# Round 0 keeps the weights' block sums of 14 quads in DRAM, and round 1 loads them

## The chip, the cores and the metric

The kernel runs on one core of one Trainium2 chip. The metric is device time in microseconds (us) of one execution, lower is better; it is given as the median of several runs. TensorE (PE in the profile) does the matmuls, VectorE (DVE), ScalarE (ACT) and GpSimd (POOL) the elementwise work, and SyncE (SP) issues nearly all DMAs, one after the other, in the order in which they stand in its queue.

## The reference

One layer: RMS norm, one input projection to eight groups of 512 columns, a gated short convolution on four of the groups, chunkwise retention with rotary positions on the other four, one output projection with a residual, and a last RMS norm. The sequence has 2048 positions behind 16 learned ones, the model is 1024 wide. Cut to what matters here:

```python
def mixer_layer(h, norm_g, w_in, conv_w, ret_norm_g, w_out, pos):
    hn = rms_norm(h, norm_g)
    proj = jnp.einsum('bld,de->ble', hn, w_in)          # 1024 -> 8*512
    cx, cb, cc, cg, q, k, v, rg = jnp.split(proj, N_PROJ, axis=-1)
    conv_out = short_conv_branch(cx, cb, cc, conv_w) * jax.nn.silu(cg)
    ...
    ret = head_group_norm(retention_chunkwise(qf, kf, vf), ret_norm_g)
    ret_out = ret.astype(h.dtype) * jax.nn.silu(rg)
    mixed = jnp.concatenate([conv_out, ret_out], axis=-1)
    return h + jnp.einsum('ble,ed->bld', mixed, w_out)
```

All of it is float32.

## The kernel before

**Rounds and units.** The 2048 positions are done in two rounds of 1024. A round has eight units: four heads of the retention (units 0 to 3, `head`) and four groups of convolution channels (units 4 to 7, `conv_group`). Round 0 goes through them in the order 4, 0, 1, 2, 3, 5, 6, 7, round 1 in the order 0 to 7. A unit has two quads, so a round has 16. After round 1 come eight pairs of the output projection (`output`).

**A quad.** A quad multiplies a 256 x 1024 piece of the weights by the 1024 x 1024 piece of x. Weights and x are each cut into 2 x 2 blocks, and the product is made in Strassen's way (the form of Winograd): seven block products instead of eight. For the weights' side that takes the four blocks a11, a12, a21, a22 (128 x 512 each, 256 KB) and four sums of them. Function `stationary` makes these in place with one addition and three subtractions: s1 = a21 + a22, a21 = a11 - a21, a11 = s1 - a11, a12 = a12 - a11. It does so on GpSimd, with one exception, the first quad of unit 0 in round 0, which DVE does. The seven left sides, in order, are a11, a12, the new a11, s1, the new a21, the new a12, a22. The weights are the same in both rounds, so before the change both rounds load the same four blocks and make the same sums.

**Split in two parts.** Each float32 operand is split into a high part (a cast on ACT to the format that TensorE takes, line 119, tile wh) and a low part (a subtraction on DVE, line 120, tile wl). Each of the seven products is 4 x 3 matmuls of 128 x 128 by 128 x 512 (line 246). The parts of the weights go through rings of 3 tiles, so the cast of one product's weights waits until PE is through with the product three places back.

**Slots.** The blocks loaded (tile ra) and s1 (tile sa) share a ring of 8 slots (`RAW`), 5 per quad. A block's load waits until the block that had the slot 8 places before is read for the last time, as a rule by its split.

**x and its sums.** The sums on the side of x are made once per round, and those for round 1 are made ahead in round 0 and kept in DRAM (`sums_x`); so are those of the output weights (`sums_w`). The first unit of round 0 (unit 4) and the first quad of unit 0 in round 1 don't use sums: they do eight plain block products (lines 327 and 303), since the sums of x aren't there yet.

**The order.** The program is written unit by unit; a scheduler then fixes one order of instructions for each engine and for SP's queue, which the chip keeps to. On SP stand, beside the weights' loads (line 542), the transposes by DMA of k, v and the retention's output (line 721, tiles pl, tr, apart, across), the loads of x, and stores of results (`mixed`, line 550). In a head, v and k go through such a transpose, are copied by ACT (lines 823 and 814), weighed (line 829) and multiplied (line 862). In round 0 the products of the 16 learned positions (line 500) read the first quad's raw blocks, so that the sums in place wait for them.

Of the kernel before, what the change touches and what calls it, by code (L numbers as in the profile page):

```python
# [8 lines left out]
F32 = mybir.dt.float32  # L9
F32R = mybir.dt.float32r  # L10
# [5 lines left out]
P = 128  # L16
# [4 lines left out]
NG = 4  # L21
EPS = 1e-6
HB = 512
# [55 lines left out]
def hybrid_trunk(ctx: ExitStack, tc: tile.TileContext, t, out: bass.AP, chunk_decay):  # L79
# [36 lines left out]
    def split(hi, lo, src, scale=None, eng=nc.vector):  # L116

        if scale is None:
            nc.scalar.copy(out=hi, in_=src)  # L119
            lowered[0] = eng.tensor_tensor(out=lo, in0=src, in1=hi.bitcast(F32), op=ALU.subtract)  # L120
            return
        scaled[0] = nc.scalar.mul(hi, src, scale)  # L122
        nc.vector.scalar_tensor_tensor(  # L123
            out=lo, in0=src, scalar=scale, in1=hi.bitcast(F32), op0=ALU.mult, op1=ALU.subtract
        )
# [12 lines left out]
            tiles.append(a)  # L138
        return tiles

    def stationary(blocks, eng=nc.gpsimd):

        a11, a12, a21, a22 = blocks
        s1 = sb.tile([P, HB], F32, name="sa", tag="ra", bufs=RAW)

        def parts(src):
            hi = sb.tile([P, HB], F32R, name="wh", tag="wh", bufs=RING)
            lo = sb.tile([P, HB], F32R, name="wl", tag="wl", bufs=RING)
            split(hi, lo, src)
            return hi, lo  # L150

        w = [parts(a11), parts(a12)]
        add(eng, s1, a21, a22)
        sub(eng, a21, a11, a21)
        sub(eng, a11, s1, a11)
        sub(eng, a12, a12, a11)
        w.append(parts(a11))
        third[0] = lowered[0]
        w += [parts(a) for a in (s1, a21)]
        fifth[0] = lowered[0]  # L160
        return w + [parts(a) for a in (a12, a22)]

    def operand(i, kt):
# [71 lines left out]
    def quad(w, m, take, steps=()):  # L235


        steps = iter(steps)

        def product(i, bank, first):  # L240
            (wh, wl) = w[i]
            for kt in range(KH):
                ks = slice(kt * P, (kt + 1) * P)
                mh, ml = m[i][kt]
                for n, (a, b) in enumerate(((wl, mh), (wh, ml), (wh, mh))):
                    nc.tensor.matmul(  # L246
                        bank, a[:, ks], b, start=first and kt == 0 and n == 0, stop=kt == KH - 1 and n == 2,
                        skip_group_check=not first,
                    )

        def copy(bank):
            c = sb.tile([P, HB], F32, name="tc", tag="tc", bufs=COPIES)
            copied[0] = nc.scalar.copy(out=c, in_=bank)  # L253
            return c

        def step():
            with tc.issue_after(copied[0].ins):
                next(steps, lambda: None)()

        xb = ps_proj()  # L260
        product(0, xb, True)
        c = copy(xb)
        step()
        yb = ps_proj()
        product(1, yb, True)
        take(0, 0, yb, c)
        product(2, xb, False)
        u2 = copy(xb)
        step()
        zb = ps_proj()  # L270
        product(3, zb, True)
        c = copy(zb)
        step()
        product(4, xb, False)
        take(1, 1, xb, c)
        product(5, zb, False)
        take(0, 1, zb, u2)
        product(6, xb, False)
        take(1, 0, xb, None)
# [258 lines left out]
        nc.tensor.transpose(tp[:, :NMETA], u, ident[:NMETA, :NMETA])  # L538
        nc.vector.tensor_copy(out=conv_carry[g], in_=tp[:, NMETA - 2 : NMETA])

    def w_loads(n):
        return [lambda a, i=i: nc.sync.dma_start(a, t["w_in"][n, i]) for i in range(4)]

    mixed = [
        dram.tile([2, 2, 2, P, KH, P], F32, name=f"mixed{b}", tag=f"mixed{b}") for b in range(SEQ // HB)
# [87 lines left out]
    def conv_group(g, r, m, f, blocks, ahead, steps=(), last=False):  # L633


        def go_on():
            next(factors_ahead[0], None)

        def behind(quad, *own):
            return [lambda n=n: (own[n](), go_on() if (quad, n) in steps else None) for n in range(3)]  # L640

        u = [gen("u") for _ in range(2)]
        rr, rr2 = ([a[:, j * HB : (j + 1) * HB] for j in range(2)] for a in f[:2])
        held = [None]

        def mul(eng, out, a, b):
            eng.tensor_tensor(out=out, in0=a, in1=b, op=ALU.mult)  # L647

        def take(i, j, pp, c):
            s = u[j][:, 2:]  # L650
            if c is None:
                mul(nc.vector, s, pp, s)
            elif i == 1:
                add(nc.vector, c, pp, c)
                held[0] = c
            else:
                add(nc.vector, s, pp, c)
                mul(nc.vector, s, s, rr2[j])
                if j == 1:
                    mul(nc.gpsimd, s, s, held[0])  # L660

        blocks, meta = blocks
        quad(stationary(blocks), m, take, behind(0, finish_late, idle, idle))
        catch_up(0)
        if meta:
            meta_carry(g, meta)
        carry(u, g, r)
        cs = [taps(u[j], g) for j in range(2)]
        gates = []

        def gated():
            j, c = gates.pop()
            nc.scalar.activation(c, c, AF.Silu)  # L673
            mul(nc.gpsimd, cs[j], cs[j], rr[j])
            mul(nc.gpsimd, cs[j], cs[j], c)

        def take(i, j, pp, c):
            if i == 0:
                add(nc.vector, c, pp, c)
                mul(nc.vector, c, c, rr[j])  # L680
                gates.append((j, c))
                if j == 1:
                    gated()
                return
            if c is not None:
                add(nc.vector, c, pp, c)
                pp = c
            taken[0] = nc.vector.tensor_tensor(out=cs[j], in0=pp, in1=cs[j], op=ALU.mult)

        n = 2 * (NG + g) + 1  # L690
        quad(stationary(load_raw(w_loads(n))), m, take, behind(1, idle, gated, idle))
        blocks = ahead()
        def store():
            for j in range(2):
                store_mixed(r, j, g, cs[j])

        if last:
            kept.append(store)
        else:
            store()  # L700
        return blocks
# [47 lines left out]
    def head(h, r, m, rot_t, f, turning, blocks, ahead, sums, first=(), between=((), idle, idle, idle)):  # L749
# [26 lines left out]
        if len(first) > 0:  # L776
            quad_plain(first[0], m, take)
        else:
            with tc.issue_after(spreading[0].ins) if r + h == 0 else nullcontext():
                w = stationary(blocks[0], nc.vector if r + h == 0 else nc.gpsimd)  # L780
            quad(w, m, take, between[0] or (finish_late,))
            catch_up(0)
        between[1]()
# [53 lines left out]
            join_keys(0)  # L837
            between[3]()

        quad(stationary(load_raw(w_loads(2 * h + 1))), m, take, (split_late, middle, late_middle))  # L840
        with tc.issue_after(copied[0].ins):
            join(1)
            weigh(1)
# [185 lines left out]
    def ahead(r, n, early=False):  # L1029

        if n is None:
            return None
        blocks = load_raw(w_loads(2 * n))
        return blocks, meta_products(blocks, early) if r == 0 else None

    warm_up(WARM)
# [171 lines left out]
```

## Time and profile before

| | |
|---|---|
| median of 3 runs | 865.88 us (865.87 to 866.58) |
| profiled execution | 866.67 us |
| its span, first to last instruction | 864.9 us |
| granted TensorE clock, mean | 0.999 |
| PE, DVE, ACT, POOL busy | 99%, 83%, 58%, 43% |
| DMA | 129.51 MB, mean 150 GB/s |

The busy time of an engine is a share of the whole span. A matmul's record lasts about 390 ns, but the records overlap, so PE's pace is read from how many matmuls start in a stretch. Round 0 ends at about 350 us, round 1 at about 700 us. In rows of groups the columns are: line, engine, operation, tiles written and read, shape, count, then busy time and mean of one (ns), then idle time of the engine ahead of them with what ended it. In rows of a timeline the first two numbers are the start in the span and the length, both in us. In rows of windows the stretch comes first, then its length, then busy time and count of PE, weight loads, DVE, ACT and POOL, then the granted clock, the share of the DMA engines and GB/s. In rows of the chain: start, length, what.

### The profile page before, as it was taken

The numbers are of one execution on the slowest core, as the hardware profiler recorded it, in microseconds if no ns is written. First come the engines' busy times: TensorE is split into PE (matmuls) and PEld (weight loads), VectorE is DVE, ScalarE is ACT, GpSimd is POOL, SyncE is SP. The second block draws the span as 40 slices with busy tenths as digits, with TensorE's granted clock in tenths as the row PEclk, the third lists the DMA queues.
The fourth block names the chain that finished last, engine by engine and source line by source line (L and its number), as shares of the span: only waits on it lengthen the run. The fifth ranks groups of instructions, "written<-read, shape, count | busy, mean of one in ns | idle before, by whom it ended". The sixth has DMA issues, their size and how long they took to land.

```text
span 864.9 us, 12698 instructions
## 1 busy us (share of the span) xinstructions
PE 854.6 (99%) x4216; PEld 705.6 (82%) x4216; DVE 716.8 (83%) x1204; ACT 499.4 (58%) x901; POOL 374.0 (43%) x278
## 2 busy tenths in 40 slices
PE   9999999999999999999999999999999999999996
PEld 6778888878887878788888888888888888788885
DVE  6798989889897977989789898988767799877663
ACT  7875648474855654948284757534433566555553
POOL 0022232423245554452232424364746455677773
PEclk9999999999999999999999999999999999999999
DMA  9724246454656533945264637546132584555441
GB/s 299 255 87 100 60 97 161 112 146 135 158 172 193 195 98 98 332 143 135 62 158 128 165 122 156 173 122 207 51 84 74 185 314 137 168 165 182 152 135 73
DMA packets 127506, 129.51 MB, mean 150 GB/s; under 512 B 58384, under 2 KB 76112, under 8 KB 127440
## 3 DMA queue, kind: packets, MB, share of 16 engines
q1 hardware_dynamic: 126864, 128.30, 49.9%
q8 instruction: 33, 0.54, 0.3%
q10 hardware_dynamic: 576, 0.40, 0.2%
q14 instruction: 33, 0.27, 0.1%
HBM read 90.91 MB, written 25.17 MB: 134 GB/s over the span
## 4 chain that ended last, share of the span: by engine, by line
PE 91%; DVE 4%; DMA 3%; issue 1%; ACT 1%; SPq 0%; POOLq 0%; POOL 0%; DVEq 0%
PE pj L246 73%; PE pj L303 5%; PE pj L327 5%; PE ms L886 2%; PE ms L875 2%; PE ms L885 2%; PE ms L862 2%; DVE wl L120 1%; PE ms L500 1%; DVE ml L120 1%; DMA ra<-in_w_in 1%; DMA w<-in_w_out 1%; DMA x<-in_xT 1%; DMA sums_w<-w 1%; DVE yo L128 0%
## 5 line engine op out<-in xcount | busy, mean ns | idle before, releaser
L246 PE MATMUL pj<-mh,wl 128*128 128x512 f32 x1008 | 395.7, 393 | 0.7 <-DVE yo L961 0.6
L246 PE MATMUL pj<-mh,wh 128*128 128x512 f32 x1008 | 393.2, 390 | 0.0
L246 PE MATMUL pj<-ml,wh 128*128 128x512 f32 x1008 | 392.7, 390 | 0.0
L119 ACT CAST wh<-ra 128x512 fp32r<-128x512 f32 x216 | 134.1, 621 | 230.8 <-PE pj L246 193.8
L120 DVE TENSOR_TENSOR wl<-ra,wh 128x512 fp32r<-128x512 f32 x216 | 192.6, 893 | 41.6 <-ACT wh L119 40.7
L246 PEld LDWEIGHTS pj<-mh,wl 128*128 128x128 f32 x1008 | 189.3, 188 | 41.8 <-issue 1.6
L246 PEld LDWEIGHTS pj<-mh,wh 128*128 128x128 f32 x1008 | 189.2, 188 | 39.5
L246 PEld LDWEIGHTS pj<-ml,wh 128*128 128x128 f32 x1008 | 189.3, 188 | 37.9
L131 POOL TENSOR_TENSOR ra<-ra 128x512 f32<-128x512 f32 x70 | 115.0, 1642 | 102.6 <-PE ms L500 51.7
L128 POOL TENSOR_TENSOR sa<-ra 128x512 f32<-128x512 f32 x35 | 53.1, 1518 | 100.1 <-DVE wl L120 42.5
L131 POOL TENSOR_TENSOR ra<-sa,ra 128x512 f32<-128x512 f32 x35 | 49.4, 1412 | 82.6 <-DVE wl L120 76.1
L253 ACT COPY tc<-pj 128x512 f32<-128x512 f32 x108 | 62.7, 581 | 0.1
L898 POOL TENSOR_TENSOR rp<-rs,neg_half 128x4 f32<-128x4 f32 x16 | 19.0, 1185 | 45.3 <-DVE rs L128 45.2
L961 DVE TENSOR_TENSOR yo<-pj,yo 128x512 f32<-128x512 f32 (+1 forms) x33 | 22.0, 671 | 16.3 <-PE pj L246 8.7
L972 POOL TENSOR_TENSOR z<-yo,final_g 128x512 f32<-128x512 f32 x16 | 27.4, 1714 | 18.6 <-DVE yo L961 18.6
L647 POOL TENSOR_TENSOR c<-c,tc 128x512 f32<-128x512 f32 x14 | 24.5, 1747 | 20.3 <-ACT tc L673 20.1
L119 ACT CAST wh<-sa 128x512 fp32r<-128x512 f32 x36 | 22.3, 619 | 18.3 <-PE pj L246 18.0
L647 POOL TENSOR_TENSOR c<-c,rr 128x512 f32<-128x512 f32 x14 | 24.1, 1718 | 19.9 <-DVE c L565 10.0
L902 DVE TENSOR_SCALAR pm<-ms,mv,rp 128x128 f32<-128x128 f32 x64 | 21.8, 404 | 10.2 <-POOL rp L898 10.2
L123 DVE SCALAR_TENSOR_TENSOR ml<-x,gain,mh 128x512 fp32r<-128x512 f32 x32 | 25.6, 836 | 5.5 <-ACT mh L122 5.4
L128 DVE TENSOR_TENSOR tc<-pj,tc 128x512 f32<-128x512 f32 x28 | 19.2, 686 | 13.1 <-PE pj L246 13.0
L120 DVE TENSOR_TENSOR wl<-sa,wh 128x512 fp32r<-128x512 f32 x36 | 27.9, 775 | 1.0 <-ACT wh L119 1.0
(161 smaller groups left out, 1256.3 us busy)
## 6 DMA issues: line engine op xcount, KB each, us to landing
ra<-in_w_in SPq DMA_DIRECT2D x124, 256.0 KB, 2.8
x<-in_xT SPq DMA_DIRECT2D x48, 256.0 KB, 5.1
w<-in_w_out SPq DMA_DIRECT2D x32, 256.0 KB, 4.9
ra<-mixed SPq DMA_DIRECT2D x32, 256.0 KB, 2.7
yo<-in_x SPq DMA_DIRECT2D x32, 256.0 KB, 4.6
ra<-in_x SPq DMA_DIRECT2D x16, 256.0 KB, 3.2
mixed<-c SPq DMA_DIRECT2D x16, 256.0 KB, 2.4
sums_x<-x SPq DMA_DIRECT2D x16, 256.0 KB, 2.7
```

The costliest lines, as they stand in the source:

```text
L119: nc.scalar.copy(out=hi, in_=src)
L120: lowered[0] = eng.tensor_tensor(out=lo, in0=src, in1=hi.bitcast(F32), op=ALU.subtract)
L123: nc.vector.scalar_tensor_tensor(out=lo, in0=src, scalar=scale, in1=hi.bitcast(F32), op0=ALU.mult, op1=ALU.subtract)
L128: eng.tensor_tensor(out=out, in0=a, in1=b, op=ALU.add)
L131: eng.tensor_tensor(out=out, in0=a, in1=b, op=ALU.subtract)
L246: nc.tensor.matmul(bank, a[:, ks], b, start=first and kt == 0 and n == 0, stop=kt == KH - 1 and n == 2, skip_group_check=not first,)
L253: copied[0] = nc.scalar.copy(out=c, in_=bank)
L303: nc.tensor.matmul(banks[i], a[:, ks], b, start=half + kt + n == 0, stop=half == 1 and kt == KH - 1 and n == 2,)
L327: nc.tensor.matmul(banks[n][i], a[:, ks], b, start=half + kt + s == 0, stop=half == 1 and kt == KH - 1 and s == 2,)
L647: eng.tensor_tensor(out=out, in0=a, in1=b, op=ALU.mult)
L961: last[0] = nc.vector.tensor_tensor(out=y[:, cs], in0=pp[:, cs], in1=y[:, cs], op=ALU.add)
L972: nc.gpsimd.tensor_tensor(out=ys[i][j], in0=y, in1=final_g[:, j * HB : (j + 1) * HB], op=ALU.mult)
```

## The change

Of the 16 quads of a round, all but the two of unit 4 are "kept" (`KEPT`, 14 quads). In round 0, `stationary` gets a place in DRAM for such a quad and, once its four sums are made, stores them there: 4 DMAs of 256 KB per quad, 56 in all, from SP. In round 1 a kept quad loads seven blocks, a11, a12, the four sums, and a22, and `stationary` only splits them: no addition or subtraction on GpSimd. The sums then aren't in a tile of their own (sa) but come in slots of the ring (ra), seven per quad instead of five. The two quads of unit 4 in round 1 still load four blocks and make their sums. The first quad of unit 0 is stored as the others are, but in round 1 it is the plain one and loads its four raw blocks, so 13 quads load sums. Lines move by up to 16 (542 is 555 in the changed kernel, 721 is 737, 550 is 566).

```diff
+    def weight_parts(src):
+        hi = sb.tile([P, HB], F32R, name="wh", tag="wh", bufs=RING)
+        lo = sb.tile([P, HB], F32R, name="wl", tag="wl", bufs=RING)
+        split(hi, lo, src)
+        return hi, lo
+
+    def stationary(blocks, eng=nc.gpsimd, keep=None):
+
+        if len(blocks) > 4:
+            return [weight_parts(a) for a in blocks]
         a11, a12, a21, a22 = blocks
         s1 = sb.tile([P, HB], F32, name="sa", tag="ra", bufs=RAW)
...
         w += [parts(a) for a in (s1, a21)]
         fifth[0] = lowered[0]
+        if keep is not None:
+            for i, a in enumerate((a11, s1, a21, a12)):
+                nc.sync.dma_start(keep[i], a)
         return w + [parts(a) for a in (a12, a22)]
...
-    def w_loads(n):
-        return [lambda a, i=i: nc.sync.dma_start(a, t["w_in"][n, i]) for i in range(4)]
+    sums_a = dram.tile([4 * NG, 4, P, HB], F32, name="sums_a", tag="sums_a")
+    KEPT = [n for n in range(4 * NG) if n // 2 != NG]
+
+    def w_loads(n, r=0):
+        if r and n in KEPT:
+            blocks = t["w_in"][n, 0], t["w_in"][n, 1], *(sums_a[n, i] for i in range(4)), t["w_in"][n, 3]
+        else:
+            blocks = [t["w_in"][n, i] for i in range(4)]
+        return [lambda a, b=b: nc.sync.dma_start(a, b) for b in blocks]
+
+    def kept_sums(n, r):
+        return sums_a[n] if r == 0 and n in KEPT else None
...
-        quad(stationary(load_raw(w_loads(n))), m, take, behind(1, idle, gated, idle))
+        quad(stationary(load_raw(w_loads(n, r)), keep=kept_sums(n, r)), m, take, behind(1, idle, gated, idle))
```

The calls in `conv_group`, `head` and `ahead` pass the round and the place in the same way.

Up to round 1 the order on PE, DVE, ACT and POOL is unchanged; SP's queue gets the stores. SP in the head of unit 1 in round 0, before (tr and pl are v and k on their way through the transpose):

```order
L542 DMA ra<-in_w_in 128x512 x3
L721 DMA_TRANSPOSE across<-apart 128x8x128
L721 DMA_TRANSPOSE tr<-pl 128x8x128
L542 DMA ra<-in_w_in 128x512
L721 DMA_TRANSPOSE tr<-pl 128x8x128
L721 DMA_TRANSPOSE across<-apart 128x8x128
L721 DMA_TRANSPOSE tr<-pl 128x8x128
L542 DMA ra<-in_w_in 128x512 x2
L721 DMA_TRANSPOSE tr<-pl 128x8x128
```

and the same place now:

```order
L555 DMA ra<-in_w_in 128x512 x3
L737 DMA_TRANSPOSE across<-apart 128x8x128
L166 DMA sums_a<-ra 128x512 x2
L737 DMA_TRANSPOSE tr<-pl 128x8x128
L555 DMA ra<-in_w_in 128x512
L737 DMA_TRANSPOSE tr<-pl 128x8x128
L737 DMA_TRANSPOSE across<-apart 128x8x128
L737 DMA_TRANSPOSE tr<-pl 128x8x128
L166 DMA sums_a<-sa 128x512
L555 DMA ra<-in_w_in 128x512 x2
L737 DMA_TRANSPOSE tr<-pl 128x8x128
```

Two stores of sums stand between the first two transposes, and one ahead of the two loads. SP from the end of round 0 into round 1, before (n are rows of x for the norm, x the blocks of round 1, t their sums):

```order
L402 DMA n<-in_x 128x512 x2
L542 DMA ra<-in_w_in 128x512 x4
L464 DMA x<-in_xT 128x512 x16
L227 DMA t<-sums_x 128x512 x3
L542 DMA ra<-in_w_in 128x512
```

and now:

```order
L408 DMA n<-in_x 128x512 x2
L166 DMA sums_a<-sa 128x512
L166 DMA sums_a<-ra 128x512
L555 DMA ra<-in_w_in 128x512 x3
L166 DMA sums_a<-ra 128x512 x2
L555 DMA ra<-in_w_in 128x512
L470 DMA x<-in_xT 128x512 x16
L233 DMA t<-sums_x 128x512 x3
L555 DMA ra<-in_w_in 128x512
```

The four stores of round 0's last quad stand among the loads of round 1's first weights, two of them ahead of the last such load and the 16 loads of x. SP in the first quads of round 1, where the loads of sums come in, before:

```order
L721 DMA_TRANSPOSE tr<-pl 128x8x128 x2
L542 DMA ra<-in_w_in 128x512 x2
L721 DMA_TRANSPOSE tr<-pl 128x8x128
L542 DMA ra<-in_w_in 128x512 x2
L721 DMA_TRANSPOSE tr<-pl 128x8x128
L542 DMA ra<-in_w_in 128x512 x7
```

and now:

```order
L737 DMA_TRANSPOSE tr<-pl 128x8x128 x2
L555 DMA ra<-in_w_in 128x512 x2
L737 DMA_TRANSPOSE tr<-pl 128x8x128
L555 DMA ra<-sums_a 128x512 x4
L737 DMA_TRANSPOSE tr<-pl 128x8x128
L555 DMA ra<-in_w_in 128x512 x3
L555 DMA ra<-sums_a 128x512 x4
L555 DMA ra<-in_w_in 128x512 x2
```

The loads of raw blocks a21 are gone, four loads of sums stand in their place, and they are ahead of the last transpose of unit 0.

More of the change, by code (lines that the diff above doesn't have):

```diff
@@ L139, in load_raw @@
         return tiles
-    def stationary(blocks, eng=nc.gpsimd):
+    def weight_parts(src):
[6 more added lines that the diff above has]
+            return [weight_parts(a) for a in blocks]
         a11, a12, a21, a22 = blocks
         s1 = sb.tile([P, HB], F32, name="sa", tag="ra", bufs=RAW)
[L146 to L150, printed above, removed]
+        parts = weight_parts
         w = [parts(a11), parts(a12)]
@@ L662, in conv_group @@
         blocks, meta = blocks
-        quad(stationary(blocks), m, take, behind(0, finish_late, idle, idle))
+        quad(stationary(blocks, keep=kept_sums(2 * (NG + g), r)), m, take, behind(0, finish_late, idle, idle))
         catch_up(0)
@@ L779, in head @@
             with tc.issue_after(spreading[0].ins) if r + h == 0 else nullcontext():
-                w = stationary(blocks[0], nc.vector if r + h == 0 else nc.gpsimd)
+                w = stationary(blocks[0], nc.vector if r + h == 0 else nc.gpsimd, kept_sums(2 * h, r))
             quad(w, m, take, between[0] or (finish_late,))
@@ L838, in late_middle @@
             between[3]()
-        quad(stationary(load_raw(w_loads(2 * h + 1))), m, take, (split_late, middle, late_middle))
+        quad(stationary(load_raw(w_loads(2 * h + 1, r)), keep=kept_sums(2 * h + 1, r)), m, take, (split_late, middle, late_middle))
         with tc.issue_after(copied[0].ins):
@@ L1032, in ahead @@
             return None
-        blocks = load_raw(w_loads(2 * n))
+        blocks = load_raw(w_loads(2 * n, r))
         return blocks, meta_products(blocks, early) if r == 0 else None
```

## The prediction

> **What bounds the kernel now.** I read the page's busy line first, then the waits of TensorE, then the chain, then the instructions around the few places where TensorE waits. The busy line and the chain:
>
> ```profile
> PE 854.6 (99%) x4216; PEld 705.6 (82%) x4216; DVE 716.8 (83%) x1204; ACT 499.4 (58%) x901; POOL 374.0 (43%) x278
> PE 91%; DVE 4%; DMA 3%; issue 1%; ACT 1%; SPq 0%; POOLq 0%; POOL 0%; DVEq 0%
> ```
>
> TensorE (PE) is at 99%, and GpSimd (POOL), which the change relieves, has 0% of the chain. A busy PE need not be at its peak, so I check its pace in a stretch of round 1, beside the waits of PE over the whole span:
>
> ```profile
> 600.00:640.00 40.00, 40.00 (x178) 33.12 (x177) 27.93 (x33) 14.77 (x25) 21.66 (x15) 1.00 0.30 88
> PE ms L1024 <- DVE warm L1016: 1.0, 1, 1.0
> PE pj L327 <- ACT mh L1069: 0.9, 1, 0.9
> PE pj L246 <- DVE yo L961: 0.6, 1, 0.6
> PE pj L303 <- DVE ml L120: 0.6, 2, 0.4
> PE pj L246 <- DVE wl L120: 0.2, 1, 0.2
> ```
>
> 178 matmuls in 40.00 us are 0.225 us each at a granted clock of 1.00, and nothing in that stretch waits. All of PE's waits add up to 3.3 us. The first two (1.9 us) lie in the opening, which the change doesn't touch. So 1.4 us are left that any relief of another engine could win: 0.16% of 865.88.
>
> **The change part by part.** I make the sum against the profiled execution, 866.67 us with a span of 864.9, which ran 0.79 above the median of 865.88; a difference found there is put on the median.
>
> *Sums no longer made in round 1.* The additions and subtractions of GpSimd from the start of round 1 to the output:
>
> ```profile
> L131 POOL TENSOR_TENSOR ra<-ra 128x512 f32<-128x512 f32 x30 | 52.8, 1759 | 27.2 <-issue 18.7 <-DVE mv L893 3.3 <-POOL c L647 2.0
> L128 POOL TENSOR_TENSOR sa<-ra 128x512 f32<-128x512 f32 x15 | 24.5, 1634 | 53.4 <-DVE wl L120 25.3 <-DMA ra<-in_w_in 16.9 <-DVE u L128 7.4
> L131 POOL TENSOR_TENSOR ra<-sa,ra 128x512 f32<-128x512 f32 x15 | 20.6, 1374 | 62.2 <-DVE wl L120 62.2
> ```
>
> These are 15 quads of 4; 13 of them load instead, so 13/15 of 97.9 us, 84.8 us, leave GpSimd. None of it is on the chain; PE's 40 us without a gap above are its cover. What it can win is the one place in round 1 where PE waits for a split of a weight:
>
> ```profile
> 594.75 1.62 POOL L131 TENSOR_TENSOR ra<-ra 128x512 f32<-128x512 f32 x1
> 595.14 1.78 DVE L647 TENSOR_TENSOR u<-u,rr 128x512 f32<-128x512 f32 x1
> 596.84 2.03 DVE L120 TENSOR_TENSOR wl<-ra,wh 128x512 fp32r<-128x512 f32 x3
> 597.11 0.39 PE L246 MATMUL pj<-mh,wh 128*128 128x512 f32 x1
> 597.67 0.47 PE L246 MATMUL pj<-mh,wl 128*128 128x512 f32 x1 [0.17 <-DVE wl L120]
> ```
>
> VectorE (DVE) comes to the split only at 596.84, behind a product that took 1.78 us while GpSimd made a sum of weights (594.75 to 596.37). The next row has the same product, 0.69 us, begun before GpSimd starts on anything. PE's starts are 0.56 apart instead of 0.225. Without the sum the split comes about 1 us earlier and the gap goes: -0.33 us. Bounds: 0 (the chain there names the landing of a store that stays) and -1.4 (every wait above goes).
>
> ```profile
> 604.66 0.69 DVE L647 TENSOR_TENSOR u<-u,rr 128x512 f32<-128x512 f32 x1
> 592.46 4.37 DMA sums_w<-w
> ```
>
> *56 stores in round 0.* No instruction of PE, DVE, ScalarE (ACT) or GpSimd changes its place before round 1; only SP gets rows. Price of one on SP and in flight, from rows of the same kind and size:
>
> ```profile
> sums_x<-x SPq DMA_DIRECT2D x16, 256.0 KB, 2.7
> ra<-in_w_in SPq DMA_DIRECT2D x124, 256.0 KB, 2.8
> tr<-pl SPq DMA_TRANSPOSE x32, 3.1
> 126.29 0.33 SPq L542 DMA_DIRECT2D ra<-in_w_in  x1
> ```
>
> 56 times 0.33 is 18.5 us of SP over 350 us, and SP mostly waits. What costs is a store that waits for GpSimd with something urgent behind it. The worst place is in the head of unit 1, where two stores now stand between two transposes:
>
> ```profile
> 120.26 1.29 POOL L131 TENSOR_TENSOR ra<-sa,ra 128x512 f32<-128x512 f32 x1 [2.74 <-DVE wl L120]
> 122.44 1.84 POOL L131 TENSOR_TENSOR ra<-ra 128x512 f32<-128x512 f32 x1 [0.89 <-POOL ra L131]
> 123.65 1.23 SPq L721 DMA_TRANSPOSE tr<-pl  x1
> 131.85 1.36 ACT L823 COPY v<-tr 128x1024 uint16<-128x1024 uint16 x1
> 142.06 0.27 ACT L531 COPY state<-ms 128x128 f32<-128x128 f32 x1 [1.05 <-PE ms L530]
> 142.96 0.71 PE L862 MATMUL ms<-v,kd 128*128 128x128 f32 x4
> ```
>
> The second store can go at 124.28 and is issued by 124.61, so the transpose starts 1.0 us later. It lands 3.1 later, at 127.7, and ACT reads it at 131.85: 4 us are the cover, and behind them 1.05 us in which ACT waits for PE. In unit 3 the same transpose moves by 0.6. The block that waits longest for its slot, the fourth of the next quad, now waits for the landing of a store too, but that store can go when its sum is made (121.55 here, landed at 124.3), before the load's old time, 126.29. So 0; if the cover were gone, 1.0 in unit 1 and 0.6 in unit 3, and nothing below 0, since a store frees nobody.
>
> *The burst between the rounds.* There the DMA engines are full, and the last store stands just ahead of the burst:
>
> ```profile
> 344.67 1.62 POOL L131 TENSOR_TENSOR ra<-ra 128x512 f32<-128x512 f32 x1 [1.97 <-issue]
> 346.91 0.33 SPq L542 DMA_DIRECT2D ra<-in_w_in  x1
> 347.29 4.70 SPq L464 DMA_DIRECT2D x<-in_xT  x10
> 350.00:362.00 12.00, 11.64 (x51) 9.32 (x51) 12.00 (x18) 11.97 (x24) 4.82 (x2) 1.00 1.01 365
> 348.70 4.39 DMA x<-in_xT
> 359.86 5.75 PE pj L303 x24
> ```
>
> The sum is made at 346.29 and the store issued by 346.62, ahead of 346.91: no issue is late. Its 262,144 bytes take 0.72 us at the 365 GB/s of the burst, and the fourth block of x that follows is on the chain to PE's wait at 359.86. Bounds 0 and +0.7; between landing and PE lie DVE instructions that are in line anyway, so I take half, +0.3.
>
> *Loads in round 1.* Each of 13 quads loads 7 blocks instead of 4, 39 more in all, through the same 8 slots. A slot is free when DVE has split the block one place earlier in the quad before:
>
> ```profile
> 606.83 1.27 DVE L120 TENSOR_TENSOR wl<-ra,wh 128x512 fp32r<-128x512 f32 x1
> 627.93 0.62 ACT L119 CAST wh<-sa 128x512 fp32r<-128x512 f32 x1 [1.48 <-PE pj L246]
> 394.74 1.24 SPq L721 DMA_TRANSPOSE tr<-pl  x1
> 406.28 0.62 ACT L119 CAST wh<-ra 128x512 fp32r<-128x512 f32 x1 [1.71 <-PE pj L246]
> ```
>
> Free at 608.1, landed at 610.9, wanted at 627.93: 17 us to spare. The tightest is the first quad of unit 1, whose sums are issued behind the transpose that ends at 395.98, landed by 398.8 and wanted at 406.28: 7 us. So 0. With that gone, a quad would wait for its own load, 2.8 us each. At the end of round 1 the third block of the output's weights now needs the split that ends at 680.90, still ahead of the load of final_g and the burst of w_out behind it, which waits for DVE until 681.5 already. Had the cover gone, every us of it would stand before the wait for the plain weights of the output (0.4 at most above):
>
> ```profile
> 680.21 0.69 DVE wl L120
> 681.53 0.33 SPq L1167
> ```
>
> *Moved work.* From the end of round 1, PE, DVE and ACT take the output's first products in another order. The work is the same; I put 0 on it, with 0.5 either way, about the larger of the waits listed there (0.6).
>
> Sum: -0.3 + 0 + 0.3 + 0 + 0 = 0.0, so 865.9 us. The ends: -1.4 - 0.5 = -1.9, and 1.6 + 0.7 + 0.5 = +2.8.
>
> **The rivals.** 0.2% (1.7 us) is about what a measurement of this kernel can tell from no change; below 864.15 is faster, above 867.61 slower.
>
> *The stores hold up round 0 (slower).* SP goes in order, so a store that waits for GpSimd holds the transposes of k and v. This decides once a transpose is late by more than the 4 us before ACT reads it, or if ACT, which runs close to full there, has in truth less room than the idle 1.05 us. Price: 1.0 + 0.6 + 0.7 of the burst = 2.3, so 868.2. For it: PE's matmul at 142.96 starts right behind ACT's last weighing. Against it: the rows above leave 4 us.
>
> *GpSimd's work was slowing DVE, and DVE the rest (faster).* For it: DVE's 1.78 beside GpSimd against 0.69 without. By this all three waits of PE behind DVE go, 1.4 us, and perhaps some 0.5 through the new order: 864.0. Against it: PE waits nowhere else, however much faster DVE gets. The Trainium skill (SBUF — State Buffer, "SBUF: two separate sides") says that GpSimd and a DVE operation with two SBUF inputs hold the shared port pair exclusively, one blocking the other for its whole instruction. The two DVE rows agree; by that rule alone DVE would gain up to 1.6 us for each sum removed.
>
> *The change moves less than it says.* Two quads of round 1 still make their sums on GpSimd, and one stored quad is never loaded back. That is 8 instructions of 60 and four stores without use, all under PE's cover: the forecast's time.
>
> **How the numbers follow.** Forecast, no difference: 0.78, of which 0.05 is the third rival. Slower: 0.16. Faster: 0.06. The time is the forecast's, 865.9. Its own range is 864.8 to 867.2. The range reaches to the slower rival's 868.2 and, below, to 864.7, most of what PE's waits allow.
>
> **What would show it.** In the changed profile: GpSimd's busy time lower by about 85 us, PE's share and its 178 matmuls in 40 us as before, the wait at a weight's split in unit 5 gone, the wait for the plain weights' split at the start of round 1 (0.4 now) grown by 0 to 0.7, SP waiting for GpSimd ahead of transposes in round 0, DVE's busy time lower by tens of us with nothing won from it. The prediction is wrong if PE shows waits for ACT at the retention's matmuls (L862) in units 1 to 3, or for splits of loaded sums in round 1, or if the pace of its matmuls itself changes.

## The result, and the profile after

The changed kernel takes 867.72 us (median of 20 runs, 866.50 to 869.20); the kernel before, run beside it on the same chip, 866.60 (865.67 to 867.64). The ratio is 1.0015, with a 95% interval of 1.0009 to 1.0022: 1.1 to 1.3 us slower, less than the 0.2% that was set as the bound of no difference (the interval ends at 0.22%), but not nothing. Put on the 865.88 of the prediction this is 867.0 to 867.2, the upper end of its range; the time of 867.72 itself lies above it, since the kernel before, too, ran 0.7 us above 865.88 here. Of the three runs of before that the prediction started from (median 865.88) two are among the lowest five of those 20.

The page of the changed kernel, its busy line and chain, then the waits of TensorE over the span (waiting line, what it waited for, us in total, times, longest):

```profile
PE 854.1 (99%) x4216; PEld 705.7 (82%) x4216; DVE 683.0 (79%) x1204; ACT 499.0 (58%) x901; POOL 288.7 (33%) x226
PE 93%; DVE 3%; issue 1%; DMA 1%; POOL 0%; ACT 0%; POOLq 0%; SPq 0%; DVEq 0%
PE pj L333 <- ACT mh L1085: 1.2, 1, 1.2
PE pj L309 <- DVE ml L120: 1.0, 1, 1.0
PE ms L1040 <- DVE warm L1032: 1.0, 1, 1.0
PE pj L252 <- DVE wl L120: 0.5, 1, 0.5
```

GpSimd is busy for 85.3 us less and VectorE for 33.8 us less. Little of it reaches the kernel's time: PE is busy for practically the same time (854.1 and 854.6), and its waits add up to 3.7 us, before 3.3. The same stretch of round 1 as before, and the place near 598 us where PE waited for a split:

```profile
600.00:640.00 40.00, 40.00 (x178) 33.15 (x177) 22.41 (x33) 14.43 (x26) 7.47 (x7) 1.00 0.45 135
595.27 0.68 DVE L663 TENSOR_TENSOR u<-u,rr 128x512 f32<-128x512 f32 x1
595.87 0.68 DVE L120 TENSOR_TENSOR wl<-ra,wh 128x512 fp32r<-128x512 f32 x1
598.86 0.39 PE L252 MATMUL pj<-mh,wl 128*128 128x512 f32 x1
```

178 matmuls in 40 us as before, with GpSimd at 7.47 us in place of 21.66 and VectorE at 22.41 in place of 27.93. The product that took 1.78 us beside a sum on GpSimd takes 0.68, and the matmul at 598.86 has no wait.

**Where the time went.** Both programs have 4,216 matmuls, in one order except for a few at the start of the output, so the n-th matmul of one execution can be set beside the n-th of the other. Against the first profile of before, the changed kernel's matmuls are later by 0.30 us after the opening (which the change doesn't touch), by 0.61 more at a split near 296 us and by 0.67 more at the split near 360. They win back 0.42 near 598 and 1.07 between 691 and 741 us. The last matmul starts at 857.42, before at 857.37. But from there to the end of the span it is 8.45 us, before 7.49: that last stretch has practically the whole 1.0 us by which the spans differ (865.9 and 864.9). What happens in it is seen in the view of the DMA queues from 861 to 868 us, and in the waits of SP. Before:

```profile
q10 hardware_dynamic: 144, 0.26, 10.1%
q1 hardware_dynamic: 149, 0.27, 9.9%
out_y<-z ACTq DMA_DIRECT2D x1, 256.0 KB, 2.8
out_y<-yo SPq DMA_DIRECT2D x1, 256.0 KB, 2.6
SPq L1204 <- DMA out_y<-yo: 2.1, 1, 2.1
```

After the change:

```profile
q10 hardware_dynamic: 144, 0.26, 10.4%
q1 hardware_dynamic: 149, 0.27, 10.1%
q14 instruction: 1, 0.01, 0.3%
out_y<-z ACTq DMA_DIRECT2D x1, 256.0 KB, 3.7
out_y<-yo SPq DMA_DIRECT2D x1, 256.0 KB, 3.5
SPq L1220 <- DMA out_y<-z: 3.1, 1, 3.1
```

The two last stores of y are issued at the same time in both (861.3), and in this stretch the queues of the data, q1 and q10, have the same 293 packets. But one packet of 8 KB of the kind "instruction" is new: a piece of an engine's program, moved by DMA as the data are. By its record it starts at 863.20 and takes 0.31 us. All packets of the stores with data but six have ended by 863.63, much as before; these six, of 2 KB each, run one behind another from 863.59 to 864.41, the first two in 0.28 and 0.23 us, where most take 0.08 or 0.09. They look like what one DMA engine had left to do behind the piece; the record doesn't name the engine. The last packets of the two stores end at 863.59 before and at 864.42 after, and nothing can hide that, for SP waits for these two landings and then the program ends. Whose program it is, and whether the other differences belong to the kernel or to one execution, is what the experiments ask.

### The profile page after: what moved, and what is told of

Same layout as the page of the kernel before. It is cut to its first block, busy times and chain, and to the rows that moved or that the text cites. A ratio compares the mean times of both kernels' runs of the same rounds, so it can differ in the third digit from the quotient of the medians.

```text
span 865.9 us, 12846 instructions
## 1 busy us (share of the span) xinstructions
PE 854.1 (99%) x4216; PEld 705.7 (82%) x4216; DVE 683.0 (79%) x1204; ACT 499.0 (58%) x901; POOL 288.7 (33%) x226
## 4 chain that ended last, share of the span: by engine, by line
PE 93%; DVE 3%; issue 1%; DMA 1%; POOL 0%; ACT 0%; POOLq 0%; SPq 0%; DVEq 0%
PE pj L252 75%; PE pj L309 5%; PE pj L333 5%; PE ms L902 2%; PE ms L891 2%; PE ms L901 2%; PE ms L878 2%; PE ms L506 1%; DVE wl L120 1%; DMA ra<-in_w_in 1%; DVE ml L123 0%; DMA gain<-in_norm_g 0%; DVE qg L931 0%; DVE x L205 0%; DVE c L581 0%
## 5 line engine op out<-in xcount | busy, mean ns | idle before, releaser
L119 ACT CAST wh<-ra 128x512 fp32r<-128x512 f32 x229 | 142.3, 621 | 250.3 <-PE pj L252 210.6
L120 DVE TENSOR_TENSOR wl<-ra,wh 128x512 fp32r<-128x512 f32 x229 | 188.3, 824 | 59.4 <-ACT wh L119 58.2
L131 POOL TENSOR_TENSOR ra<-ra 128x512 f32<-128x512 f32 x44 | 69.0, 1567 | 78.7 <-PE ms L506 38.3
L128 POOL TENSOR_TENSOR sa<-ra 128x512 f32<-128x512 f32 x22 | 33.2, 1508 | 59.2 <-DMA ra<-in_w_in 38.2
L131 POOL TENSOR_TENSOR ra<-sa,ra 128x512 f32<-128x512 f32 x22 | 31.7, 1440 | 30.5 <-DVE wl L120 20.6
L663 POOL TENSOR_TENSOR c<-c,rr 128x512 f32<-128x512 f32 x14 | 22.3, 1592 | 36.9 <-DVE c L704 25.0
L128 POOL TENSOR_TENSOR yo<-yo,tc 128x512 f32<-128x512 f32 x18 | 26.0, 1454 | 3.4 <-ACT tc L259 3.2
L581 DVE SCALAR_TENSOR_TENSOR c<-u,conv_w,c 128x512 f32<-128x512 f32 x32 | 25.2, 830 | 2.3 <-POOL u L572 1.2
```

Of the source, the lines that this page charges most:

```text
L128: eng.tensor_tensor(out=out, in0=a, in1=b, op=ALU.add)
L131: eng.tensor_tensor(out=out, in0=a, in1=b, op=ALU.subtract)
L581: nc.vector.scalar_tensor_tensor(out=c, in0=u[:, tap : tap + HB], scalar=conv_w[:, g, tap : tap + 1], in1=c, op0=ALU.mult, op1=ALU.add)
```

## The experiments

The table has what the profile of each kernel shows at three splits that PE waits for, as the distance from the start of one matmul to the start of the next (0.226 us where nothing waits), and the end from the start of the last matmul. "Groups" are the six stored quads of units 5 to 7, "heads" the eight of units 0 to 3.

| kernel | stores | loads | near 296 | near 360 | near 598 | end |
|---|---|---|---|---|---|---|
| before | none | no | 0.24 | 0.74 | 0.56 | 7.49 |
| before, second profile | none | no | 0.35 | 1.39 | 0.75 | 7.48 |
| before, VectorE's program longer | none | no | 0.42 | 1.41 | 0.41 | 8.39 |
| stores of the heads | heads | no | 0.30 | 0.75 | 0.88 | 7.42 |
| loads alone | none | yes | 0.92 | 1.41 | 0.23 | 7.54 |
| the change | all | yes | 0.86 | 1.41 | 0.23 | 8.45 |
| the change, second profile | all | yes | 1.79 | 1.41 | 0.23 | 8.46 |
| the change, VectorE's program longer | all | yes | 0.77 | 1.37 | 0.23 | 7.48 |
| stores alone | all | no | 1.65 | 1.40 | 0.62 | 7.47 |
| stores of the groups | groups | no | 1.55 | 1.41 | 0.49 | 7.47 |
| stores of the groups less quad 12 | 20 | no | 1.35 | 1.39 | 0.41 | 7.78 |
| stores of quad 12 | 4 | no | 0.72 | 0.75 | 0.40 | 7.76 |
| mended | all less quad 12 | yes | 0.55 | 1.40 | 0.23 | 7.43 |

### The stores alone

The loads of round 1 are those of before, so GpSimd makes the sums again:

```diff
-        if r and n in KEPT:
-            blocks = t["w_in"][n, 0], t["w_in"][n, 1], *(sums_a[n, i] for i in range(4)), t["w_in"][n, 3]
-        else:
-            blocks = [t["w_in"][n, i] for i in range(4)]
+        blocks = [t["w_in"][n, i] for i in range(4)]
```

> Round 0 stores the sums as in the change, round 1 makes them on GpSimd as before and loads nothing back; every engine but SP has the order of before. If the trace of the change is read rightly, the stores alone cost what they showed there: about +0.6 at a split near 296 us and +0.7 at the plain split near 361 us, and the waits near 598, 696 and 740 us stay: the last matmul some 1.2 us later than before's 857.4, the end behind it 7.5 us long as before, the time about 867.8. If the two waits in round 0 were chance of one execution, the last matmul is within 0.3 of before's and the time is 866.6 to 866.9. If the forecast of the prediction holds (burst alone, half a store), +0.3: 866.9 and one wait grown, near 361.

Measured: 867.72 us beside 866.15 of before, 1.6 us more; ratio 1.0015 (1.0006 to 1.0024). The last matmul comes 1.25 us later than before's, though the opening was 0.9 us shorter in this execution, with an end of 7.47. So the stores do cost something: 0.5 to 2.1 us by the interval. In the profile it stands near 296 and 360 us, as expected; how much of that belongs to the stores and how much to the execution is told further down.

### The loads alone

```diff
-            blocks = t["w_in"][n, 0], t["w_in"][n, 1], *(sums_a[n, i] for i in range(4)), t["w_in"][n, 3]
+            blocks = t["w_in"][n, 0], t["w_in"][n, 1], *(t["w_in"][n, i] for i in range(4)), t["w_in"][n, 3]
...
-        if keep is not None:
-            for i, a in enumerate((a11, s1, a21, a12)):
-                nc.sync.dma_start(keep[i], a)
```

> Round 0 stores nothing; round 1 loads seven blocks for each of the 13 quads, but the four in the place of the sums are blocks of w_in themselves, so the products of round 1 are made of other numbers. Every engine but SP has the order of the change. If relief of GpSimd and the new order win what the change's trace showed, the waits near 598, 696 and 740 us are gone or small (-0.4, -0.3, -0.7) and the last matmul is about 1.4 us earlier than before's, near 856.0. VectorE's program keeps its 39 more waits, so by the theory of its last program load the end behind the last matmul is 8.4 us and the time about 866.2; if that end came from the stores or their tensor, it is 7.5 and the time 865.2. If the waits of round 1 went only because the stores had moved the phases, they are back, and the time is 866.6 or more.

Measured: 865.41 us beside 866.15, 0.7 us less; ratio 0.9993 (0.9984 to 1.0002), so a gain that is likely and not certain. The distance near 598 is the usual 0.23. The last matmul starts at 856.97, 0.40 earlier than before's and not the expected 1.4, and the opening alone was 0.75 us shorter here. The end is the usual one too, 7.54, against the expectation: with 1,598 entries in VectorE's program (all entries of the trace, its semaphore waits with them) a piece of program was still loaded at 865.6, when the span (864.5) was already over. Whose piece that is, the record doesn't say; the stores alone, with 1,564 entries, have such a late one too. And the starts near 296 and 360 us are as late here as in the change (0.92 and 1.41), with no store in the program. That was the first sign that I had taken waits of one execution for waits of the change.

### VectorE's program made longer, in the change and in before

Writes of one column to a tile that nobody reads, in the output, where VectorE has room: 20 in the change, 42 in the kernel before. PE, ScalarE, GpSimd and SP keep their orders.

```diff
+        with tc.issue_after(last[0].ins):
+            for _ in range(PAD.get(pair, 0)):
+                nc.vector.memset(pad, 0.0)
```

> The change with 20 writes of one column added to VectorE's program in the output, where it has room; no other engine's order moves. By the theory that the change costs 0.9 us at the end because VectorE's program grew by 42 entries and its last 8 KB load falls among the last stores, that load now comes over 10 us earlier, the end behind the last matmul is 7.5 us instead of 8.4, and the time 0.9 less than the change's: 866.8. If the end is long for another reason (where the tensors lie, the number of stores), nothing moves: 867.7.

> The kernel before with 42 writes of one column added to VectorE's program in the output, as many entries as the change adds; no other engine's order moves, and nothing is stored or loaded. By the theory of the last program load, an 8 KB load falls among the last stores here too: the end behind the last matmul 8.4 us instead of 7.5, the time 0.9 over before's: 867.5. If the end of the change is long for another reason, nothing moves: 866.6.

Measured: the change with 20 more 866.38 us beside 866.15 (ratio 1.0001, 0.9993 to 1.0010), where the change itself stood 1.1 over before. Before with 42 more 866.78 beside 866.15 (1.0006, 0.9997 to 1.0015): by its median 0.6, with the expected 0.9 inside the interval and nothing not ruled out. The traces decide it. From 861 us to the end, the change with 20 more:

```profile
q1 hardware_dynamic: 144, 0.26, 9.7%
q10 hardware_dynamic: 144, 0.26, 9.5%
SPq L1225 <- DMA out_y<-z: 2.2, 1, 2.2
```

and before with 42 more:

```profile
q1 hardware_dynamic: 144, 0.26, 10.0%
q10 hardware_dynamic: 144, 0.26, 9.9%
q14 instruction: 1, 0.01, 0.3%
SPq L1209 <- DMA out_y<-yo: 3.0, 1, 3.0
```

The piece of program comes and goes with the length of VectorE's program, and with it 0.9 to 1.0 us of the end, whatever is stored or loaded. VectorE has 1,560 entries before and 1,602 in the change; the 42 are semaphore waits, 39 of them in round 1, as many as there are more loads. At 1,602 the last piece is loaded at 863.2 (the change) and 862.7 (before with 42 more), among the last stores. At 1,622 none comes after 859.6.

### Which stores cost, and what a second profile of before shows

`KEPT` in the kernel with the stores alone is cut down:

```diff
-    KEPT = [n for n in range(4 * NG) if n // 2 != NG]
+    KEPT = [n for n in range(4 * NG) if n < 2 * NG]
```

and, for the groups, `if n >= 2 * NG + 2`.

> As the stores alone (round 1 makes its sums itself), but only the 8 quads of units 0 to 3, the heads, store: 32 of the 56. The heads of units 1 and 3 are where the prediction put the danger (a store that waits for GpSimd ahead of the transposes). In every profile so far TensorE runs from 24 to 290 us in step with before, to 0.1 us, with or without stores. So by the theory that the stores' cost sits in the convolution groups this kernel takes 0.0 to +0.3 over before; by the rival that any store costs by its bytes, 32/56 of the 1.6 us that 56 cost, +0.9.

> As the stores alone, but only the 6 quads of units 5 to 7, the convolution groups, store: 24 of the 56. By the theory that the cost sits there (a store that waits for GpSimd on SP pushes the stores of c and of sums_x and so the landing of the next blocks and of x, with VectorE full up to the split near 296 us): +1.0 to +1.6 over before, the start at the split near 296 us late by 0.5 to 1.4. By the rival of bytes, 24/56 of 1.6, +0.7. If the 1.6 of all stores was chance of the executions, both kernels are within 0.4 of before.

> The kernel before itself, a second profile, to see which waits a second execution repeats. If the waits of the first profile belong to the kernel, 0.0 near 296, 0.5 over the usual start near 360, 0.3 near 598, 0.4 near 696 and 0.7 near 740 us come again. If they are set by when the transfers of the bursts land in one execution, the waits near 296 and 360 us come out up to 0.7 larger with nothing changed, as they did in the kernel that only shifts VectorE's program, and 0.66 of the growth near 360 us is no cost of the store.

Measured: the heads 866.49 us, the groups 867.30, before 866.38. The ratios, 1.0004 (0.9995 to 1.0013) and 1.0003 (0.9995 to 1.0012), don't tell them apart; the traces do. With the heads' stores PE goes, from the opening on, in step with before to 290 us, within 0.1 us, and starts 0.30 after its predecessor near 296. With the groups' stores it starts 1.55 after. The second profile of before, and the kernel with the heads' stores:

```profile
PE pj L303 <- DVE ml L120: 1.0, 1, 1.0
```

```profile
PE pj L309 <- DVE ml L120: 0.6, 2, 0.4
```

The wait for the plain weights near 360 us is 1.0 us in the first, with nothing changed, and 0.4 in the second. Of the thirteen profiles ten have the long distance there (1.37 to 1.41) and three the short one (0.74 or 0.75). It is one of two outcomes of an execution, and the rows near 350 us show what the two are. First the short outcome, then the long one, both of the kernel before:

```profile
350.65 0.69 DVE L120 TENSOR_TENSOR wl<-sa,wh 128x512 fp32r<-128x512 f32 x1
350.15 2.34 POOL L647 TENSOR_TENSOR c<-c,rr 128x512 f32<-128x512 f32 x1 [1.64 <-DVE c L565]
```

```profile
350.46 1.78 DVE L120 TENSOR_TENSOR wl<-sa,wh 128x512 fp32r<-128x512 f32 x1
349.96 1.74 POOL L647 TENSOR_TENSOR c<-c,rr 128x512 f32<-128x512 f32 x1 [1.64 <-DVE c L565]
```

A split on VectorE and a product on GpSimd meet there. In the three short profiles the split takes 0.68 or 0.69 us and the product 2.34, in the ten long ones the split 1.78 or 1.79 and the product 1.73 or 1.74; counted from the same matmul, both start at the same times to 0.02 us in all thirteen. So one or the other goes first, and VectorE comes out of it 0.66 us later or not. From there to the split near 360 us it has no idle time in any profile, so that wait isn't set by when a transfer lands, though I had expected that. With the last quad's store just ahead of the burst all seven are long, without it three of six. So the store isn't what makes the long one; that it makes it likelier, which would be 0.33 us in the mean, can't be told from so few.

### Four stores, their complement, and a mended version

> Only the four stores of the first quad of unit 6 (number 12), whose last two are ready late: SP stands before them until GpSimd has made the sums, and the stores of c and of sums_x queue behind. All else as before. By the theory that this is where the group stores cost, the start at the split near 296 us is late by 0.5 to 1.4 beside at most 0.7 without group stores, the landing of the first block of the next quad comes 0.4 to 0.7 later after its issue, and the time is 0.5 to 1.0 over before. If it takes all 24 (their bytes in the burst near 270 us), the split near 296 us is late by 0.0 to 0.2 and the time as before.

> The complement: the group stores without the quad numbered 12, 20 stores. By the theory of the held queue, the split near 296 us is late by 0.0 to 0.7, as without stores, and the time within 0.4 of before. By the bytes in the burst ahead of it: late by 0.5 to 1.4, and the time up to 1.0 over before.

The third kernel, the mended one, is the change with 20 more writes on VectorE and with

```diff
-    KEPT = [n for n in range(4 * NG) if n // 2 != NG]
+    KEPT = [n for n in range(4 * NG) if n // 2 != NG and n != 2 * NG + 4]
```

> The change without the quad numbered 12 (neither stored nor loaded: round 1 makes its sums itself) and with the 20 writes of one column in VectorE's program, so that its last load falls ahead of the last stores. If both costs are named rightly, the shifted change (0.2 over before) less the 0.75 of the split near 296 us: 0.5 under before, the end behind the last matmul 7.5 us, the wait near 598 us gone. If the stores' cost isn't that quad's, 0.2 over before again.

> The change itself, a second profile. If the load of VectorE's program at the end belongs to the program and not to the execution, it comes again behind the last matmul (near 863) and the end is 8.4 us again. The starts near 296 and 360 us are late by 0.5 to 1.4 and by 0.0 or 0.66 again, as an execution has it; the wait near 598 us stays gone.

Measured: 867.39 and 867.17 us beside 866.65, with ratios of 1.0004 (0.9995 to 1.0013) and 1.0005 (0.9996 to 1.0014): nothing that the times can tell. What happens on SP is plain in the timeline. Before:

```profile
285.61 0.38 SPq L550 DMA_DIRECT2D mixed<-c  x1
286.71 0.33 SPq L215 DMA_DIRECT2D sums_x<-x  x1
287.85 0.37 SPq L550 DMA_DIRECT2D mixed<-c  x1
288.40 0.37 SPq L542 DMA_DIRECT2D ra<-in_w_in  x1
```

After the change:

```profile
282.85 3.93 SPq L166 DMA_DIRECT2D sums_a<-ra  x2
286.88 0.39 SPq L566 DMA_DIRECT2D mixed<-c  x1
287.36 0.52 SPq L221 DMA_DIRECT2D sums_x<-x  x1
288.16 0.37 SPq L566 DMA_DIRECT2D mixed<-c  x1
288.72 0.47 SPq L555 DMA_DIRECT2D ra<-in_w_in  x1
```

SP stands before the second store of quad 12 until GpSimd has made its sum, and is past it at 286.8. The store of `mixed`, which was ready, goes out 1.3 us later than before (1.0 when the 0.3 by which this execution is late is taken off), and the store of sums_x behind it 0.65. Before, the store of `mixed` had landed at 287.9; now it lands at 289.5, and its traffic meets that of a load of weights at 288.72, which itself is in time. That load lands after 3.63 us in place of 2.92. The profiles split cleanly on this: with the four stores of quad 12 (six profiles) it takes 3.49 to 3.65 us, without them (seven) 2.92 to 3.19. Behind it waits GpSimd with the next quad's first sum. Rows around 292 us, first of the kernel with the heads' stores, then of the change:

```profile
291.71 1.24 DVE L928 SCALAR_TENSOR_TENSOR qg<-apart,ret_g,qg 128x512 f32<-128x512 f32 x1
291.10 1.30 POOL L128 TENSOR_TENSOR sa<-ra 128x512 f32<-128x512 f32 x1 [1.73 <-DMA ra<-in_w_in]
```

```profile
292.52 1.78 DVE L931 SCALAR_TENSOR_TENSOR qg<-apart,ret_g,qg 128x512 f32<-128x512 f32 x1
292.47 1.29 POOL L128 TENSOR_TENSOR sa<-ra 128x512 f32<-128x512 f32 x1 [2.29 <-DMA ra<-in_w_in]
296.76 0.47 PE L252 MATMUL pj<-mh,wl 128*128 128x512 f32 x1 [0.47 <-DVE wl L120]
```

The later sum begins with VectorE's operation, which then takes 1.78 us; the earlier one was half over when the operation began, and it took 1.24. By the Trainium skill (SBUF — State Buffer, "SBUF: two separate sides") a GpSimd operation that reads SBUF and an operation of VectorE with two inputs in SBUF, as this one has, share a pair of ports, and the one that starts first has it for its whole instruction while the other waits. These rows agree: 1.29 us of GpSimd from 292.47 is over at 293.76, and VectorE's operation ends 0.55 us behind that, in the first pair of rows 0.55 behind 292.40 too. It takes 1.65 to 1.81 us in the six profiles with quad 12's stores and 1.19 to 1.38 in the other seven, and VectorE, which has no idle time there, brings that half microsecond to the split that PE waits for.

Counted from a matmul ahead of it and beside the first profile of before, VectorE falls back by 0.46 to 0.62 us in this one operation with quad 12's stores, and by 0.00 to 0.19 without them: 0.46 us between the means.

That isn't all of it, though, and here my theory fell short. Without quad 12's stores the other 20 still had 1.35 us near 296:

```profile
296.90 0.47 PE L252 MATMUL pj<-mh,wl 128*128 128x512 f32 x1 [0.96 <-DVE wl L120]
```

and the loads alone had 0.92 with no store at all. What else makes VectorE late there goes back to a block of x that ScalarE waits for near 273 us, ahead of the cast that VectorE's next split needs. The row of it in the first profile of the change, then in the second:

```profile
273.47 0.72 ACT L208 ACTIVATE x<-x,gain 128x512 f32<-128x512 f32 x1 [2.95 <-DMA x<-in_xT]
```

```profile
273.62 0.72 ACT L208 ACTIVATE x<-x,gain 128x512 f32<-128x512 f32 x1 [4.11 <-DMA x<-in_xT]
```

In eight profiles ScalarE waits 2.85 to 3.71 us here, and VectorE is at most 0.11 us later at 290 us than in the first profile of before, counted beside PE. In the other five (the loads alone, the second profile of the change, the stores alone, those of the groups, and those of the groups less quad 12) it waits 3.77 to 4.22, and VectorE is 0.68 to 1.04 later; part of that is a split near 283 us that takes 1.56 to 1.71 us beside a product on GpSimd, and 1.17 or 1.18 in the eight. This and the loss in the operation above make up the whole column near 296 us, to 0.01. The late block came in four of the seven profiles with the other groups' stores and in one of the six without, and the change itself had both outcomes; whether those stores make it likelier stays open.

The mended kernel takes 865.73 us beside 866.65 of before: ratio 0.9989 (0.9980 to 0.9997), 0.9 us faster by the medians, where 0.5 was expected, and the only kernel here whose interval lies wholly below 1. Its end is 7.43 us, its distances near 296 and 598 are 0.55 and 0.23, and its waits are

```profile
PE pj L309 <- DVE ml L120: 1.0, 1, 1.0
PE ms L1045 <- DVE warm L1037: 1.0, 1, 1.0
PE pj L333 <- ACT mh L1090: 0.9, 1, 0.9
PE pj L252 <- DVE wl L120: 0.2, 1, 0.2
```

The second profile of the change (867.87 us) has its piece of program at 863.4 and an end of 8.46 us, so that cost belongs to the program and not to one execution.

## Why the prediction was right, and where it was not

The forecast was no difference, by a sum of 0.0 us, and the change came out 1.1 us slower: inside the bound, and at the upper end of the range. That the sum was near is in part luck: the stores were put at nothing and four of them cost 0.46 us, the +0.3 of the burst rested on a mechanism that isn't there, and the main cost was in no step at all.

- *Sums no longer made in round 1, -0.33.* Right, in place and in size. All five profiles with loads have 0.23 us near 598; the eight without have 0.40 to 0.88, 0.57 in the mean, so the gain is 0.34. GpSimd lost 85.3 us where 84.8 were worked out.
- *56 stores in round 0, 0.* Failed for four of them. In the heads, where I put the danger, the cover held: PE doesn't move. I looked for a late transposition there and took the units behind them for harmless without reading what stands behind each store on SP. In unit 6's first quad that is the store of `mixed`, and through it the landing of a load, a sum on GpSimd and a full VectorE: 0.46 us in the mean. With all of the groups' stores the distance near 296 is 1.32 us in the mean of five profiles, without any 0.45 in five; but three of the first five had the late block of x and one of the second, so the rest of this 0.9 isn't shown to be the stores'. SP stood before stores for GpSimd as the prediction said it would:

```profile
SPq L166 <- POOL ra L131: 75.2, 34, 8.6
```

- *The burst between the rounds, +0.3.* The mechanism failed. The wait there grew from 0.4 to 1.0, within the bound that was given, and by the first two profiles I would have called it confirmed; that was luck. VectorE is in line from 350 us to that split without a pause, so neither a landing of x nor the store's bytes set the wait, and the second profile of before has the same growth without a store. What sets it is whether VectorE's split or GpSimd's product goes first at 350 us. What is left is that the long wait came in seven of seven profiles with the store and in three of six without, 0.33 us in the mean.
- *Loads in round 1, 0.* Right: the margins of 7 to 17 us held. Only at the end of round 1, near 693 us, did two of the five profiles with loads start a product some 0.35 us late.
- *Moved work, 0 with 0.5 either way.* Right in size. From 691 to 741 us the five profiles with loads are 0.7 us shorter than the first of before, in the mean, and the seven others without them 0.5; about 0.2 goes with the loads.
- *What the sum lacked: the end, +0.96.* I counted the instructions that the change adds to SP's queue and looked at VectorE only for its order, in which the waits don't show. The 39 loaded blocks give VectorE a semaphore wait more each, so its last piece of program falls among the last stores. This is practically the whole difference that was measured: without it the change is 0.2 us from before (866.38 and 866.15).

Added up from what the profiles show, -0.34, -0.2, 0.46 and 0.96 make +0.9 us, an estimate beside the 1.1 to 1.3 measured; what the stores may add by making a late block or the long wait likelier would come on top. The range of the prediction doesn't fit its own words: 864.8 to 867.2 reaches neither up to 868.2 nor down to 864.7.

Of the rivals, the one in which the stores hold up round 0 had the right mechanism, SP's order, at the wrong place; its 868.2 wasn't reached. The one in which GpSimd slows VectorE is borne out in its mechanism (0.68 us in place of 1.78) and not in its price: VectorE lost 33.8 us of work, and PE got back the one wait at 598 and some of those in the output. That two quads still make their sums and one is stored for nothing was not tested apart; no wait of PE points to it.

## What to carry to other kernels

Where TensorE is at 99%, work taken off another engine is worth the few waits that PE still has; here 0.3 us of 85, and the transfers that replace it must be followed through their queue: what stands behind each store in SP's order, and which load that traffic then meets. Before two profiles are subtracted from each other, take a second one of the unchanged kernel: where two engines meet, it can come out either way, here worth 0.66 us with nothing changed, and so can the landing of a block behind a burst of loads. And look at the kernel's last microseconds apart from the rest: if the end has become longer, see whether a piece of a program is loaded among the last stores; a few idle instructions, more or fewer, move it away.

## What the runs showed of the hardware that I had not expected

A program's own loading can cost time. Programs come in pieces while they run, in the change 33 of 16,384 bytes in one queue (q8) and 34 of 8,192 in another (q14), through the DMA engines that also carry the data; one such piece among the last two stores makes the kernel's end 0.9 to 1.0 us longer than in the same kernel without it (8.39 to 8.46 us in three profiles of kernels with 1,602 entries on VectorE, 7.42 to 7.78 in ten others). The Trainium skill (Runtime: NRT & Kernel Launch, "Instruction fetch mechanics") says that a sequencer fetches the next block of its program through a DMA queue of its own while it runs, at a cost that is mostly hidden. The trace agrees for the pieces in the middle of the span, in that the waits of PE listed above name VectorE and ScalarE alone, and not for this last one.

The split near 360 us has two outcomes, a distance of 0.75 or of 1.4 us between two matmuls, with nothing in between, and the kernel before showed the one in its first profile and the other in its second. They are the two orders in which GpSimd's product and VectorE's split can go at 350 us; what chooses between them, when both start at the same times to 0.02 us, wasn't found.
